# A lone tile's pass given ten load buffers and six split pairs, with the other tiles' first norm moved into routing

## The chip, the cores and the metric

One core of a Trainium2 chip runs the whole kernel. The metric is the device time of one execution in microseconds (us). Engines are called TensorE (PE in rows), VectorE (DVE), ScalarE (ACT), GpSimd (POOL) and the sync engine (SP), whose in-order queue issues nearly all weight loads. A name with a q behind it (SPq, ACTq) is an engine's queue of DMA issues and semaphore steps.

## The reference, cut to what matters

The input is 512 tokens of 2048 features in fp32, with 256 memory tokens. One layer is computed:

```python
h = rmsnorm(x, norm_mix_g); m = rmsnorm(mem, norm_mem_g)
z = h @ w_in                       # 2048 x 12288: u|v, conv B|C|h, queries, 3 x 2048 gates
y_A = u * (mask(W_s) @ LN(v) + b)  # u, v after gelu; per 128-token block
y_B = B * causal_conv3(C * h)
y_C = softmax(q k^T / 16) v        # 4 heads over the 256 memory tokens
x = x + (sum_n sigmoid(g_n) * (y_n @ w_branch[n])) @ w_out
h = rmsnorm(x, norm_ffn_g)
idx, g = product_key_top16(h @ w_q, keys)   # 8 heads x 16 of 16384 experts
x = x + sum_k g_k * gelu(w_down[idx_k] . h) * w_up[idx_k]
out = rmsnorm(x, norm_final_g)
```

## The kernel before, in words

Tokens are four tiles of 128. Every weight matrix streams from memory in units of 128 x 1024 fp32 (512 KB). `halves` (line 92) yields them. In the mixer each unit is split for an fp32-accurate product: ScalarE rounds `raw` to `whi` (line 111), VectorE subtracts to get `wlo` (line 112), and `mm3` (line 115) issues three matmuls, hi x hi, hi x lo and lo x hi, for each 128 rows of the unit. The tags `raw`, `whi` and `wlo` of the pool A have 4, 3 and 3 buffers. A load waits until the VectorE split has read the buffer that it reuses. In memory and routing the weights are not split (`raw=True`): there the fp32 unit goes to TensorE as it is, and its loads rotate through all three tags.

The order of the work is:

1. `memory` (line 227): keys and values of the 256 memory tokens, fp32 matmuls. In it `load_x(0)` (line 281) loads tile 0, squares it on ScalarE, multiplies by 1/rms and the gain on VectorE (line 298, gain broadcast to all partitions in `gb`), transposes it on TensorE (line 302) and splits it into `h0`.
2. `first_tile` (line 469): the lone tile's pass, called so because tile 0 goes through the mixer alone. Its tokens are the stationary operand and a weight row of 512 columns moves (`chainN`, line 175), six matmuls of 512 columns for each unit. The order is queries, attention, merge 2, gate input, u, merge 0, conv, merge 1, w_out: 272 units. In three places (`hooks`, lines 409, 413, 446) `load_x(1)`, `load_x(2)` and `load_x(3)` norm, transpose and split the other tiles into `hiT` and `loT`, 2 x 24 KB of each partition, in a pool `half` (H) that is open from the start. After w_out comes routing for tile 0 (line 509): four groups of eight w_q units, and after each group the scores and the top 16.
3. `other_tiles` (line 541): tiles 1 to 3 through the mixer together, from `hiT` and `loT`; then `retrieval` (routing and gates of the other tiles, down projections) and `experts` (line 806), whose up projections I call the up stage. There a pool `exp` gives two further buffers for each of `raw`, `whi` and `wlo`; before the change units 0 and 1 of each five took those. Beside stages 3 and later, single expert rows are gathered by GpSimd and multiplied on VectorE, paced by the units.

Every projection of the lone tile (line 317) ends with a ScalarE copy (line 327) of four 128-column chunks that TensorE then transposes (line 330). A scheduler fixes the order of the instructions on each engine and queue when the kernel is built, from the order in the program and modelled durations; on the chip each engine runs its list in order. Pools hand out a buffer when it is free in that plan.

Of the kernel before, what the change touches and what calls it, by code (L numbers as in the profile page):

```python
# [9 lines left out]
F32 = mybir.dt.float32  # L10
F32R = mybir.dt.float32r
# [4 lines left out]
AF = mybir.ActivationFunctionType  # L16
# [3 lines left out]
P = 128  # L20
# [42 lines left out]
class Builder:  # L63
    def __init__(self, ctx, tc, a):
        self.ctx, self.tc, self.nc, self.a = ctx, tc, tc.nc, a
        self.n_unit, self.n_down, self.extra = 0, 0, None
        self.gth, self.last_lo = None, None
# [24 lines left out]
    def halves(self, src, raw=False):  # L92


        nc, A = self.nc, self.A
        for u in range(src.shape[-1] // 1024):
            self.n_unit += 1
            if raw:
                tag, bufs = (("raw", 4), ("wlo", 3), ("raw", 4), ("wlo", 3), ("raw", 4), ("wlo", 3), ("raw", 4),
                             ("whi", 3))[self.n_unit % 8]  # L100
                w = A.tile([P, 1024], F32, tag=tag, name="unit", bufs=bufs)
                nc.sync.dma_start(w, src[:, bass.ts(u, 1024)])
                yield (w,)
# [5 lines left out]
            hi = pool.tile([P, 1024], F32R, tag="whi", name="whi", bufs=b or 3)  # L109
            lo = pool.tile([P, 1024], F32R, tag="wlo", name="wlo", bufs=b or 3)  # L110
# [83 lines left out]
    def consts(self):  # L194
        nc, A, a = self.nc, self.A, self.a
        self.ident = A.tile([P, P], F32, tag="ident", name="ident")
        make_identity(nc, self.ident)
        self.iota = A.tile([P, P], F32, tag="iota", name="iota")
        nc.gpsimd.iota(self.iota, pattern=[[1, P]], base=0, channel_multiplier=0,
                       allow_small_or_imprecise_dtypes=True)  # L200
        self.ss = A.tile([P, NT, 4], F32, tag="ss", name="ss")
        self.rg = A.tile([P, 1], F32, tag="rg", name="rg")
        self.fg = A.tile([P, KC], F32, tag="fg", name="fg")
        nc.scalar.dma_start(self.fg, a["ffn_g"])

    def small_operands(self):
# [20 lines left out]
    def memory(self):  # L227
# [24 lines left out]
        for c in range(WC):  # L252
# [20 lines left out]
            if c == 1:  # L273
                self.load_x(0)
        for c in range(2):
# [5 lines left out]
    def load_x(self, t):  # L281

        nc, A = self.nc, self.A
        x = self.rows("x", [P, D])
        nc.sync.dma_start(x, self.a["x"][bass.ts(t, P), :])
        if t == 0:
            self.gb = A.tile([P, D], F32, tag="hg", name="gb", bufs=1)
            nc.scalar.dma_start(self.gb, row_bcast(self.a["norm_mix_g"], D))
            self.h0 = [self.rows("h0", [P, KC, P], F32R) for _ in range(2)]
        elif t == 1:  # L290
            self.hiT = self.H.tile([P, KC, ND * P + P], F32R, tag="h", name="hiT", bufs=2)
            self.loT = self.H.tile([P, KC, ND * P + P], F32R, tag="h", name="loT", bufs=2)
        ss = self.small("sx", 4)
# [3 lines left out]
        r = self.rstd_of(ss[:, None, :])  # L297
        nc.vector.scalar_tensor_tensor(x, x, r, self.gb, op0=ALU.mult, op1=ALU.mult)
        for k4 in range(KC // 4):
            p = self.bank2("pt").rearrange("p (k t) -> p k t", k=4)  # L300
            for k in range(4):
                nc.tensor.transpose(p[:, k, :], x[:, bass.ts(k4 * 4 + k, P)], self.ident)
            hi, lo = self.h0 if t == 0 else (self.hiT, self.loT)
            s = (slice(None), slice(4 * k4, 4 * k4 + 4), bass.ts(max(t - 1, 0), P))
            self.split(hi[s], lo[s], p)


    def mixer(self, act, hooks):

# [60 lines left out]
        for h in range(HEADS):  # L370
# [32 lines left out]
            for c in range(2):  # L403
# [4 lines left out]
                put(2 * h + c, po)  # L408
        hooks[0]()
        merge(2, y, True)  # L410


        hooks[1]()
        vt = [M.tile([P, W], F32, tag="v", name="vt", bufs=4) for _ in range(nt)]
# [30 lines left out]

        hooks[2]()
        y, put = new_y()
# [21 lines left out]
    def first_tile(self):  # L469

        nc, A, a = self.nc, self.A, self.a
        act = Act(P, hi=lambda k: self.h0[0][:, k, :], lo=lambda k: self.h0[1][:, k, :])
        merged = self.mixer(act, [lambda: self.load_x(1), lambda: self.load_x(2), lambda: self.load_x(3)])
# [14 lines left out]
        for c in range(4):  # L488
# [52 lines left out]
    def other_tiles(self):  # L541
        nc, tc, A, a = self.nc, self.tc, self.A, self.a
        n = ND * P + P
        act = Act(n, hi=lambda k: self.hiT[:, k, :], lo=lambda k: self.loT[:, k, :])
        none = lambda: None
        merged = self.mixer(act, [none, none, none])
        self.gh = gh = self.H.tile([P, KC, n], F32R, tag="h", name="gh", bufs=2)
# [258 lines left out]
    def experts(self):  # L806
# [80 lines left out]
    def run(self):  # L887
        nc, tc = self.nc, self.tc
        self.h2h = None
        self.open()  # L890
        self.hpool, self.mpool = ExitStack(), ExitStack()
        self.H = self.hpool.enter_context(tc.tile_pool(name="half", bufs=1, side="right", reuse_waits="tile"))
        self.M = self.mpool.enter_context(tc.tile_pool(name="mix", bufs=1, side="left", reuse_waits="tile"))
# [26 lines left out]
def layout(inputs):  # L920
# [6 lines left out]
        "norm_mix_g": a["norm_mix_g"][0],  # L927
        "mem_g": cols(a["norm_mem_g"][0], KC),
        "ffn_g": cols(a["norm_ffn_g"][0], KC),
        "norm_ffn_g": a["norm_ffn_g"][0],  # L930
# [40 lines left out]
```

## Time and profile before

| | us |
|---|---|
| median of 3 runs | 4021.7 (4014.24 to 4022.86) |
| the profiled execution, its own time | 4022.7 |
| its span | 4020.8 |
| TensorE busy, whole span | 3603.0 (90%) |
| VectorE busy, whole span | 3157.9 (79%) |
| ScalarE busy, whole span | 1586.4 (39%) |
| lone tile's pass, first to last split matmul | 131.0 to 687.5 |
| routing of tile 0 | about 696 to 761 |

In rows of instructions the line comes first, then engine, operation, output<-inputs and shape; then busy us in total and mean ns of one; behind the bar the idle time of the engine just before them, with what ended it. TensorE's matmul rows are pipelined: the start of one and the next tell its pace, their lengths overlap.

### The profile page before, as it was taken

How to read it: one execution, taken by the hardware profiler on the slowest of the kernel's cores; microseconds unless marked ns; L12 is line 12 of the kernel's file. 1: busy time of each engine (PE TensorE's matmuls, PEld its weight loads, DVE VectorE, ACT ScalarE, POOL GpSimd, SP SyncE). 2: the span in 40 equal slices, each digit the busy share in tenths (PEclk: the TensorE clock that was granted, in tenths of full speed). 3: DMA queues.
4: the chain of work that ended last, by engine and by line, in shares of the span. 5: the costliest groups of instructions: out<-in, count | busy, mean ns of one | idle time of the engine just before them, and what ended most of it. 6: DMA issues, size and time to landing. Idle time of an engine off the chain costs nothing.

```text
span 4020.8 us, 52410 instructions
## 1 busy us (share of the span) xinstructions
PE 3603.0 (90%) x19846; PEld 3173.8 (79%) x19846; DVE 3157.9 (79%) x4050; ACT 1586.4 (39%) x2175; POOL 731.1 (18%) x544
## 2 busy tenths in 40 slices
PE   9888788989999999999689889999997788888888
PEld 6555555979999999998589888999997566666666
DVE  1566766588788888888897999888877787887887
ACT  1565655133233232323423355455433333333333
POOL 0000000022121132122200211222221222222231
PEclk9999999999999999999799999999998998999999
DMA  6587878589989999999754899999999989989996
GB/s 225 181 273 256 271 263 297 190 313 342 346 333 341 338 353 347 349 338 375 292 203 141 304 327 329 366 350 347 363 373 364 338 317 330 341 314 333 326 328 227
DMA packets 318653, 1240.83 MB, mean 309 GB/s; under 512 B 32704, under 2 KB 98240, under 8 KB 248768
## 3 DMA queue, kind: packets, MB, share of 16 engines
q1 hardware_dynamic: 242800, 692.16, 49.3%
q0 software_dynamic: 73728, 536.90, 35.2%
q10 hardware_dynamic: 1872, 8.43, 0.6%
q8 instruction: 155, 2.54, 0.2%
q14 instruction: 98, 0.80, 0.1%
HBM read 1198.56 MB, written 38.80 MB: 308 GB/s over the span
## 4 chain that ended last, share of the span: by engine, by line
PE 48%; DVE 21%; DMA 20%; issue 5%; ACT 5%; POOL 0%; ACTq 0%; SPq 0%; DVEq 0%; POOLq 0%
DVE wlo L112 9%; DMA raw<-in_w_upN 7%; DVE xg L777 4%; DMA raw<-in_w_restN 4%; ACT whi L111 4%; PE pg L117 3%; PE pg L118 3%; PE pg L119 3%; DMA raw<-in_w_downT 3%; PE pd L119 3%; PE po L118 3%; PE pd L117 3%; PE pd L118 2%; PE po L119 2%; PE po L117 2%
## 5 line engine op out<-in xcount | busy, mean ns | idle before, releaser
L111 ACT ACTIVATE whi<-raw 128x1024 fp32r<-128x1024 f32 x1096 | 1154.1, 1058 | 1873.6 <-DMA raw<-in_w_upN 347.7
L112 DVE TENSOR_TENSOR wlo<-raw,whi 128x1024 fp32r<-128x1024 f32 x1096 | 1335.0, 1222 | 461.2 <-ACT whi L111 457.4
L119 PE MATMUL pd<-h2h,wlo 128*128 128x256 f32 x2048 | 596.4, 291 | 46.3 <-DVE wlo L112 45.6
L774 POOL DMA_INDIRECT row<-in_w_down,eidx x256 | 333.3, 1302 | 1532.1 <-DVE row L779 976.1
L777 DVE SCALAR_TENSOR_TENSOR xg<-row,dots,xg 128x2048 f32<-128x2048 f32 x256 | 600.9, 2347 | 13.4 <-DMA row<-in_w_up,eidx 8.6
L779 DVE SCALAR_TENSOR_TENSOR row<-row,hg 128x2048 f32<-128x2048 f32 x256 | 585.0, 2286 | 25.3 <-DMA row<-in_w_down,eidx 25.1
L117 PE MATMUL pd<-h2h,whi 128*128 128x256 f32 x2048 | 591.6, 289 | 8.4 <-ACT ga L698 6.2
L774 POOL DMA_INDIRECT row<-in_w_up,eidx x256 | 385.0, 1504 | 1152.7 <-DVE xg L777 1042.5
L118 PE MATMUL pd<-h2l,whi 128*128 128x256 f32 x2048 | 585.7, 286 | 0.0
L118 PE MATMUL po<-wlo,aw 128*128 128x512 f32 x1024 | 430.5, 420 | 103.3 <-DVE wlo L112 102.9
L117 PE MATMUL po<-whi,aw 128*128 128x512 f32 x1024 | 395.8, 411 | 69.7 <-ACT whi L111 69.7
L119 PEld LDWEIGHTS pd<-h2h,wlo 128*128 128x128 f32 x2048 | 398.9, 195 | 65.0 <-DVE wlo L112 64.6
L119 PE MATMUL po<-whi,aw 128*128 128x512 f32 x1024 | 419.7, 410 | 0.0
L117 PEld LDWEIGHTS pd<-h2h,whi 128*128 128x128 f32 x2048 | 399.4, 195 | 10.8 <-ACT ga L698 7.4
L118 PEld LDWEIGHTS pd<-h2l,whi 128*128 128x128 f32 x2048 | 399.5, 195 | 0.0
L118 PEld LDWEIGHTS po<-wlo,aw 128*128 128x128 f32 x1024 | 205.1, 200 | 182.9 <-DVE wlo L112 140.3
L117 PEld LDWEIGHTS po<-whi,aw 128*128 128x128 f32 x1024 | 202.3, 199 | 122.8 <-ACT whi L111 79.0
L117 PE MATMUL pg<-hiT,whi 128*128 128x384 f32 x768 | 259.9, 338 | 2.0 <-ACT whi L111 2.0
L119 PE MATMUL pg<-hiT,wlo 128*128 128x384 f32 x768 | 259.8, 338 | 0.6 <-DVE wlo L112 0.6
L118 PE MATMUL pg<-loT,whi 128*128 128x384 f32 x768 | 259.3, 338 | 0.0
L119 PEld LDWEIGHTS po<-whi,aw 128*128 128x128 f32 x1024 | 204.9, 200 | 41.7
L124 DVE TENSOR_TENSOR aw<-ga,aw 128x256 fp32r<-128x256 f32 x128 | 53.9, 423 | 139.3 <-ACT aw L123 138.9
(352 smaller groups left out, 5912.6 us busy)
## 6 DMA issues: line engine op xcount, KB each, us to landing
raw<-in_w_downT SPq DMA_DIRECT2D x256, 512.0 KB, 6.6
raw<-in_w_upN SPq DMA_DIRECT2D x256, 512.0 KB, 7.1
raw<-in_w_restN SPq DMA_DIRECT2D x176, 512.0 KB, 5.0
raw<-in_w_rest SPq DMA_DIRECT2D x176, 512.0 KB, 6.9
raw<-in_w_out SPq DMA_DIRECT2D x72, 512.0 KB, 6.7
raw<-in_w_branchN SPq DMA_DIRECT2D x48, 512.0 KB, 5.4
raw<-in_w_branch SPq DMA_DIRECT2D x48, 512.0 KB, 7.5
raw<-in_w_gv SPq DMA_DIRECT2D x32, 512.0 KB, 5.9
```

Of the source, the lines that this page charges most:

```text
L111: nc.scalar.activation(hi, w, AF.Copy)
L112: self.last_lo = nc.vector.tensor_sub(lo, w, hi.bitcast(F32)).ins
L117: mm(out, lh, rh, start=start, stop=False)
L118: mm(out, lh, rl, start=False, stop=False)
L119: mm(out, ll, rh, start=False, stop=stop)
L124: (lo_engine or self.nc.vector).tensor_sub(lo, src, hi.bitcast(F32))
L774: nc.gpsimd.indirect_dma_start(out=row, out_offset=None, in_=self.a["w_up" if up else "w_down"], in_offset=bass.IndirectOffsetOnAxis(ap=g. ...
L777: nc.vector.scalar_tensor_tensor(g.x, row, g.dots[:, k:k + 1], g.x, op0=ALU.mult, op1=ALU.add)
L779: nc.vector.scalar_tensor_tensor(row, row, 1.0, g.hg, op0=ALU.mult, op1=ALU.mult, accum_out=g.dots[:, k:k + 1])
```

## The change

Before the first tile's pass a pool `first` is opened on the side and in the size (48 KB of each partition) of the two tiles `hiT` and `loT`; it holds six `raw` buffers and three pairs of `whi` and `wlo`. It is closed after the last w_out unit, and only then the pool for `hiT` and `loT` is opened. Units take the new pool's `raw` for 6 of each 10, and its split pairs for 3 of each 6. In the up stage the two numbers are 2 of each 6 for `raw` and 2 of each 5 for the splits.

`load_x` is cut in two. `load_x` itself loads and scales by 1/rms on ScalarE; `turn_x` transposes, multiplies by the gain on VectorE (gain now a value per partition, `mixg`), and splits. Tile 1 is loaded when w_out begins, into the second buffer of the tag y beside tile 0's x; tiles 2 and 3 are loaded in routing, into the same two buffers; tiles 1, 2 and 3 are turned after the first, second and third group of w_q units.

```diff
-            x = self.extra is not None and self.n_unit % 5 < 2
-            pool, b = (self.extra, 2) if x else (A, 0)
-            w = pool.tile([P, 1024], F32, tag="raw", name="raw", bufs=b or 4)
+            X, nr, ns = self.extra
+            pool, b = (X, nr) if self.n_unit % (nr + 4) < nr else (A, 4)
+            w = pool.tile([P, 1024], F32, tag="raw", name="raw", bufs=b)
             nc.sync.dma_start(w, src[:, bass.ts(u, 1024)])
+            pool, b = (X, ns) if self.n_unit % (ns + 3) < ns else (A, 3)
...
             if c == 1:
-                self.load_x(0)
+                x = self.load_x(0)
+            if c == 3:
+                self.turn_x(0, x)
...
     def load_x(self, t):
-        x = self.rows("x", [P, D])
+        x = self.rows("x", [P, D]) if t == 0 else A.tile([P, D], F32, tag="y", name="x", bufs=2)
...
-        nc.vector.scalar_tensor_tensor(x, x, r, self.gb, op0=ALU.mult, op1=ALU.mult)
+        for c in range(4):
+            xs = x[:, bass.ts(c, 512)]
+            nc.scalar.activation(xs, xs, AF.Copy, scale=r)
+        return x
+
+    def turn_x(self, t, x):
...
         for k4 in range(KC // 4):
             p = self.bank2("pt").rearrange("p (k t) -> p k t", k=4)
             for k in range(4):
-                nc.tensor.transpose(p[:, k, :], x[:, bass.ts(k4 * 4 + k, P)], self.ident)
-            self.split(hi[s], lo[s], p)
+                self.nc.tensor.transpose(p[:, k, :], x[:, bass.ts(k4 * 4 + k, P)], self.ident)
+            ks = slice(4 * k4, 4 * k4 + 4)
+            h = self.tmp("h3").rearrange("p (k t) -> p k t", k=4)
+            self.nc.vector.tensor_tensor(h, p, self.mixg[:, ks, None].to_broadcast([P, 4, P]), op=ALU.mult)
+            s = (slice(None), ks, bass.ts(max(t - 1, 0), P))
+            self.split(hi[s], lo[s], h)
...
         mh, ml = (self.rows("m0", [P, KC, P], F32R) for _ in range(2))
+        xs1 = self.load_x(1)
...
         nc.sync.dma_start(self.xdram, x)
+        self.xpool.close()
+        self.extra = None, 0, 0
+        self.H = self.hpool.enter_context(self.tc.tile_pool(name="half", bufs=1, side="right", reuse_waits="tile"))
...
+        xs = [None, xs1, self.load_x(2), None]
         for h4 in range(4):
             pq = self.bank("pq")
             for s in range(4):
                 self.whole(pq[:, bass.ts(s, P)], a["w_q"][4 * h4 + s], act)
+            if h4 < 3:
+                self.turn_x(h4 + 1, xs[h4 + 1])
+            if h4 == 0:
+                xs[3] = self.load_x(3)
...
-            self.extra = L
+            self.extra = L, 2, 2
...
+        X = self.xpool.enter_context(tc.tile_pool(name="first", bufs=1, side="right", reuse_waits="tile"))
+        self.extra = X, 6, 3
```

The three hooks of the mixer are taken out.

## Rows read from the trace of the kernel before

**Rows 1.** Busy time by stretch: engines' busy us (count), clock, DMA share, GB/s.

```profile
10.00:20.00 10.00, 8.10 (x36) 6.25 (x35) 6.68 (x19) 4.83 (x8) 0.00 (x0) 0.83 1.03 412
...
131.00:688.00 557.00, 457.73 (x1810) 326.47 (x1808) 386.13 (x447) 337.61 (x418) 4.39 (x16) 0.97 0.80 264
...
696.00:761.00 65.00, 62.09 (x542) 61.33 (x542) 16.36 (x98) 7.31 (x12) 0.00 (x0) 0.99 0.70 234
3080.00:3960.00 880.00, 731.68 (x2877) 566.32 (x2878) 719.00 (x733) 295.25 (x368) 230.61 (x126) 0.93 0.91 329
```

**Rows 2.** Chain that ended last, 632 to 660: start us, length, what.

```profile
634.61 5.01 DMA raw<-in_w_out
...
639.73 1.07 ACT whi L111
640.82 1.24 DVE wlo L112
642.07 4.77 DMA raw<-in_w_out
```

**Rows 3.** Waits of the sync queue, 131 to 688: total us, times, longest.

```profile
SPq L108 <- DVE wlo L112: 376.7, 236, 9.3
```

**Rows 4.** Timeline of TensorE, 669 to 671.6: start us, length, instruction.

```profile
669.06 0.39 PE L118 MATMUL po<-wlo,m 128*128 128x512 f32 x1
...
671.55 0.39 PE L117 MATMUL po<-whi,m 128*128 128x512 f32 x1
```

**Rows 5.** Instruction groups by form, 131 to 688, TensorE (columns: section above).

```profile
L118 PE MATMUL pg<-wlo,h 128*128 128x512 f32 x192 | 82.0, 427 | 20.9 <-DVE wlo L112 20.0
...
L383 PE MATMUL sc<-kT,qT 128*128 128x256 f32 x16 | 5.1, 449 | 0.0
L406 PE MATMUL po<-pT,vm 128*128 128x128 f32 x32 | 4.5, 283 | 0.7 <-ACT pT L402 0.7
L436 PE MATMUL sv<-wT,vt 128*128 128x128 f32 x16 | 3.3, 373 | 0.0
...
L330 PE MATMUL put<-ident,pur 128*128 128x128 f32 x8 | 1.8, 361 | 6.8 <-ACT pur L327 6.8
```

**Rows 6.** Timelines of TensorE, memory (29 to 33) and routing (728 to 744).

```profile
28.64 2.75 PE L167 MATMUL pk<-mT,unit 128*128 128x256 f32 x12
31.44 1.09 PE L302 MATMUL pt<-ident,x 128*128 128x128 f32 x8
...
728.04 1.16 PE L517 MATMUL sc<-keys,qT 128*128 128x128 f32 x8 [0.69 <-ACT qT L514]
729.04 14.46 PE L167 MATMUL pq<-hgT,unit 128*128 128x128 f32 x128
```

**Rows 7.** DMA queues, 131 to 688: packets, MB, share of 16 engines.

```profile
q1 hardware_dynamic: 39329, 144.79, 78.3%
```

**Rows 8.** Instruction groups by form, 131 to 688, VectorE and ScalarE.

```profile
L112 DVE TENSOR_TENSOR wlo<-raw,whi 128x1024 fp32r<-128x1024 f32 x269 | 327.3, 1224 | 148.0 <-ACT whi L111 145.1 <-PE pb L119 0.2
L111 ACT ACTIVATE whi<-raw 128x1024 fp32r<-128x1024 f32 x269 | 283.4, 1058 | 205.6 <-DMA raw<-in_w_restN 79.9 <-DMA raw<-in_w_branchN 28.0 <-DMA raw<-in_w_out 21.1
...
L295 ACT ACTIVATE junk<-x 128x512 bf16<-128x512 f32 x12 | 7.4, 616 | 0.0
L298 DVE SCALAR_TENSOR_TENSOR x<-x,r,gb 128x2048 f32<-128x2048 f32 x3 | 7.0, 2349 | 0.1
```

**Rows 9.** Lines 596, 590: duration ns min/median/max, first and last start us.

```profile
L596 DVE TENSOR_TENSOR h<-pt,fg x12: 684/691/692, 1963.0 to 2001.9; 128x512 f32<-128x512 f32 x12
...
L590 ACT ACTIVATE h<-x,r x12: 705/706/722, 1961.1 to 1998.4; 128x512 f32<-128x512 f32 x12
```

**Rows 10.** Waits of the sync queue, 3080 to 3960.

```profile
SPq L108 <- DVE wlo L112: 238.6, 127, 7.1
```

**Rows 11.** DMA issues, 3080 to 3960: count, KB each, median us to landing.

```profile
raw<-in_w_upN SPq DMA_DIRECT2D x238, 512.0 KB, 7.1
```

More of the change, by code (lines that the diff above doesn't have):

```diff
@@ L65, in __init__ @@
         self.ctx, self.tc, self.nc, self.a = ctx, tc, tc.nc, a
-        self.n_unit, self.n_down, self.extra = 0, 0, None
+        self.n_unit, self.n_down, self.extra = 0, 0, (None, 0, 0)
         self.gth, self.last_lo = None, None
@@ L104, in halves @@
                 continue
-            x = self.extra is not None and self.n_unit % 5 < 2
-            pool, b = (self.extra, 2) if x else (A, 0)
-            w = pool.tile([P, 1024], F32, tag="raw", name="raw", bufs=b or 4)
+            X, nr, ns = self.extra
+            pool, b = (X, nr) if self.n_unit % (nr + 4) < nr else (A, 4)
+            w = pool.tile([P, 1024], F32, tag="raw", name="raw", bufs=b)
             nc.sync.dma_start(w, src[:, bass.ts(u, 1024)])
-            hi = pool.tile([P, 1024], F32R, tag="whi", name="whi", bufs=b or 3)
-            lo = pool.tile([P, 1024], F32R, tag="wlo", name="wlo", bufs=b or 3)
+            pool, b = (X, ns) if self.n_unit % (ns + 3) < ns else (A, 3)
+            hi = pool.tile([P, 1024], F32R, tag="whi", name="whi", bufs=b)
+            lo = pool.tile([P, 1024], F32R, tag="wlo", name="wlo", bufs=b)
             nc.scalar.activation(hi, w, AF.Copy)
@@ L204, in consts @@
         nc.scalar.dma_start(self.fg, a["ffn_g"])
+        self.mixg = A.tile([P, KC], F32, tag="mixg", name="mixg")
+        nc.scalar.dma_start(self.mixg, a["mix_g"])
     def small_operands(self):
@@ L283, in load_x @@
         nc, A = self.nc, self.A
-        x = self.rows("x", [P, D])
+        x = self.rows("x", [P, D]) if t == 0 else A.tile([P, D], F32, tag="y", name="x", bufs=2)
         nc.sync.dma_start(x, self.a["x"][bass.ts(t, P), :])
[L286 to L292, printed above, removed]
         ss = self.small("sx", 4)
@@ L297, in load_x @@
         r = self.rstd_of(ss[:, None, :])
-        nc.vector.scalar_tensor_tensor(x, x, r, self.gb, op0=ALU.mult, op1=ALU.mult)
+        for c in range(4):
[3 more added lines that the diff above has]
+    def turn_x(self, t, x):
+        if t == 0:
+            hi, lo = self.h0 = [self.rows("h0", [P, KC, P], F32R) for _ in range(2)]
+        elif t == 1:
+            self.hiT = self.H.tile([P, KC, ND * P + P], F32R, tag="h", name="hiT", bufs=2)
+            self.loT = self.H.tile([P, KC, ND * P + P], F32R, tag="h", name="loT", bufs=2)
+        if t > 0:
+            hi, lo = self.hiT, self.loT
         for k4 in range(KC // 4):
@@ L301, in load_x, with mixer @@
             for k in range(4):
-                nc.tensor.transpose(p[:, k, :], x[:, bass.ts(k4 * 4 + k, P)], self.ident)
-            hi, lo = self.h0 if t == 0 else (self.hiT, self.loT)
-            s = (slice(None), slice(4 * k4, 4 * k4 + 4), bass.ts(max(t - 1, 0), P))
-            self.split(hi[s], lo[s], p)
-    def mixer(self, act, hooks):
+                self.nc.tensor.transpose(p[:, k, :], x[:, bass.ts(k4 * 4 + k, P)], self.ident)
[4 more added lines that the diff above has]
+            self.split(hi[s], lo[s], h)
+    def mixer(self, act):
         nc, A, M, a = self.nc, self.A, self.M, self.a
@@ L408, in mixer @@
                 put(2 * h + c, po)
-        hooks[0]()
         merge(2, y, True)
-        hooks[1]()
         vt = [M.tile([P, W], F32, tag="v", name="vt", bufs=4) for _ in range(nt)]
@@ L443, in mixer @@
         merge(0, y, False)
-        hooks[2]()
         y, put = new_y()
@@ L472, in first_tile @@
         act = Act(P, hi=lambda k: self.h0[0][:, k, :], lo=lambda k: self.h0[1][:, k, :])
-        merged = self.mixer(act, [lambda: self.load_x(1), lambda: self.load_x(2), lambda: self.load_x(3)])
+        merged = self.mixer(act)
         x = A.tile([P, D], F32, tag="y", name="x0", bufs=2)
@@ L544, in other_tiles @@
         act = Act(n, hi=lambda k: self.hiT[:, k, :], lo=lambda k: self.loT[:, k, :])
-        none = lambda: None
-        merged = self.mixer(act, [none, none, none])
+        merged = self.mixer(act)
         self.gh = gh = self.H.tile([P, KC, n], F32R, tag="h", name="gh", bufs=2)
@@ L890, in run @@
         self.open()
-        self.hpool, self.mpool = ExitStack(), ExitStack()
-        self.H = self.hpool.enter_context(tc.tile_pool(name="half", bufs=1, side="right", reuse_waits="tile"))
+        self.hpool, self.mpool, self.xpool = ExitStack(), ExitStack(), ExitStack()
+        X = self.xpool.enter_context(tc.tile_pool(name="first", bufs=1, side="right", reuse_waits="tile"))
+        self.extra = X, 6, 3
         self.M = self.mpool.enter_context(tc.tile_pool(name="mix", bufs=1, side="left", reuse_waits="tile"))
@@ L928, in layout @@
         "mem_g": cols(a["norm_mem_g"][0], KC),
+        "mix_g": cols(a["norm_mix_g"][0], KC),
         "ffn_g": cols(a["norm_ffn_g"][0], KC),
```

## The prediction, made before the changed kernel was run

> **What bounds the kernel now.** I read the busy time by stretch first, then the waits of the sync queue, the chain of waits, the groups of instructions by form, and short timelines.
>
> The lone tile's pass runs from the first w_restN matmul at 131.0 us to the last w_out matmul at 687.5 us: 556.5 us. In that stretch no engine and no queue is full: TensorE is shown busy 82%, VectorE 69%, ScalarE 61%, DMA share 0.80 at 264 GB/s [rows 1]. What repeats is a loop through four load buffers. The chain shows it unit by unit: a load of 5.01 us, its ScalarE split of 1.07, its VectorE split of 1.24, and at once the next load into the buffer just released, 7.46 us after the one before [rows 2]. Four buffers in 7.46 us are 1.87 us a unit, 281 GB/s. The sync queue confirms it: its weight loads wait 376.7 us in 236 waits for the VectorE split that empties their buffer [rows 3]. The pass has 272 units of 512 KB (from the code: 80 for projections and gate input, 144 in the three merges, of which 48 branch units, 16 more for queries and 32 of w_out), so it runs at 2.05 us a unit; 0.18 of that is other waits.
>
> How far it can fall is set by the next limits. TensorE: a unit is six matmuls of 512 columns, and twelve of them issue 2.49 us apart from first to last, eleven intervals of 0.2264 us [rows 4]; 272 x 6 x 0.2264 = 369.5 us. Its other work is scores, attention output and spatial gating, at most 5.1 + 4.5 + 3.3 us by their busy rows [rows 5], and 64 transposes at 1.09/8 = 0.136 us [rows 6], 8.7 us: 391 us with those. The 48 transposes of the other tiles are another 6.5. So TensorE is really idle 556.5 - 391 - 6.5 = 159 us, not the 99 us that its busy row leaves.
>
> The Trainium skill (Perfetto Trace Analysis, Identifying the Most-Contended Engine) says that matmul busy time is a poor measure of headroom because matmuls are pipelined, and sends the reader to weight-load time. The trace agrees: rows of 390 ns start every 0.226 us, and weight loads fill 59% of the stretch. By the busy row alone the pass could lose at most 99 us.
>
> Loads: the queue moves 144.79 MB in the pass [rows 7], two of them for x tiles 2 and 3, and at 412 GB/s, which the first units of the kernel reach with the same 4 KB rows and more buffers [rows 1], this takes 351 us. VectorE has 386 us busy [rows 1], less 19 for what leaves it (three multiplies of 2.35, twelve half-size splits of some 0.7 and small operations): 367 us. So behind the buffer limit stand TensorE at 391, VectorE at 367 and the loads at 351.
>
> **The change part by part.**
>
> Buffers in the pass. Load buffers go from 4 to 10, split pairs from 3 to 6, in even rotation (6 of 10 and 3 of 6 in the new pool). The loop of 7.46 us then allows 0.75 us a unit, so the wait for a load buffer is gone as a limit and loads lengthen until another limit holds. The split pairs would have been next: a pair is held for 1.06 + 1.22 [rows 8] + 6 x 0.226 = 3.64 us and some hand-overs, over three 1.2 to 1.3 us, over six 0.6. What is late next is TensorE. It also starts with more units ready, since ten loads and six splits can wait for it during the memory stage, where it is fully busy.
>
> New length of the pass: 391 us of TensorE work, plus ten places where a projection is copied by ScalarE before it is transposed. Each costs at least what the same copy costs in routing, 0.69 us [rows 6], and about half a split queued ahead: 12 us together. That is 403 us, the low end. High end: half of the remaining idle time stays (159 - 12 = 147, half 74): 477 us. I take 430 us, 1.58 us a unit: 143 MB in that time is 332 GB/s, next to the 329 GB/s which this kernel holds over 880 us of its up stage, where three resources are as evenly loaded as they will be here [rows 1]. Gain 126 us, between 79 and 153.
>
> The Trainium skill (HBM Reference, Specifications (TRN2)) gives a core some 358 GB/s as its share of a memory that two cores use, and more when it streams alone. By the share the loads alone would need 400 us, just above TensorE, and I would put the pass at about 440, 10 us less gain. The trace speaks against the share here: 412 GB/s over 10 us.
>
> Norms of tiles 1 to 3 taken out of the pass. Per tile that is one VectorE multiply of 2.35 us, four ScalarE squares of 0.62 [rows 8], splits, 16 transposes and a 1 MB load. VectorE and ScalarE hide it once they aren't the limit, so it is already in the figures above; TensorE's 6.5 us were left out of the 391. One tile (1) comes back at the pass's end, its load beside that of tile 0: both wait for the last branch's y, and behind them on the sync queue wait w_out loads. 1 MB is 2.5 us at 412 GB/s; loads already issued into ten buffers cover it. On ScalarE four squares and four scaled copies of 0.71 [rows 9] fall among 32 splits: 32 x 1.06 + 5.3 and the rest is near TensorE's 43.5 us. I leave it within the 27 us allowed above 403.
>
> Turning tiles 1 to 3 during routing. Routing is TensorE-bound: groups of 128 fp32 matmuls in 14.46 us, nothing between them but a 0.69 us wait for the copy before the scores [rows 6]. Each tile adds 16 transposes, 2.2 us, in two PSUM buffers. The third four wait for the VectorE multiply by the gain, 0.69 us [rows 9], and that and the split (0.69 more, as the multiply) make about 1.3 us per four: 2.5 to 4 us a tile. The 0.69 us wait is then filled. Three tiles: +8 us. VectorE's own 12 multiplies and 12 splits, 17 us, lie in time in which it is a quarter busy [rows 1]. Low end 0, if the transposes fall into gaps. High end +35: the load of tile 3 waits until tile 1 is transposed, and if w_q loads stand behind it on the in-order sync queue, TensorE finds its buffers empty for a load's length, 5 to 8 us at each of three places.
>
> The first tile in the memory stage: its gain is now applied after the transposes, on VectorE, beside TensorE-bound matmuls; a 1 MB broadcast load goes and an 8 KB one comes. I take 0, +-2 us, since the eight transposes stand between matmuls with no gap [rows 6]. Opening the other tiles' space later: its first writer comes in routing, its first reader after, 0; without that cover it would be one release wait, under 1 us.
>
> Up stage. The same lines now rotate loads there through 6 of 6, where before two in five units had a distance of 5 and the others of 6 to 8. The queue is in order, so the effective depth goes from about 5.6 to 6. Its loads wait 238.6 us for a split to empty a buffer [rows 10] and take 7.1 us [rows 11]; DMA is at 0.91, VectorE at 82% [rows 1]. 7% more depth on those 238.6 us is 17 us at most unless the stage reorders; against DMA's remaining 9%, I take -12. Ends: -35 (DMA share from 0.91 to 0.95 over 880 us) and +15 (the gathers and the small loads are squeezed by earlier weight loads).
>
> Sum: -126 + 8 - 12 = -130 us. The profiled execution took 4022.7 us (span 4020.8): 4022.7 - 130 = 3892.7; the median of the three runs is 1.0 lower, so 3892 us.
>
> **The rivals.**
> A. The buffers deepen but the orders written at build time, or loads and TensorE limits that nearly coincide, keep half or more of the idle time. For it: at 1.36 us a unit the loads would have to run at 385 GB/s, 94% of the best row, and VectorE would be 85% full (367 of 430) with splits that depend on ScalarE. Against: six pairs are 8 us of lead. Pass 477 to 500, routing +15, up -5: 3935 to 3965, say 3948.
> B. All limits are met: pass 403 to 410, up stage -30, routing +5: about 3848.
> C. Slower. Engines run in a fixed order. With six pairs free, splits of later units may be queued on ScalarE ahead of the copies, sigmoids and exponentials that TensorE waits for. Up to six splits are 6.4 us; there are 38 such places (10 copies, 12 sigmoids, some 16 of attention and gating). From 3.4 us each the gain of 130 is gone; at 5 us it is 190 us, so 4080. For it: a copy's wait is already 6.8 us in two places [rows 5]. Against: those waits arise now because the splits ahead wait for loads, which end.
> D. The change doesn't do what it says: loads lengthen in proportion to their number, the rate stays at 264 GB/s and the pass at some 550, routing +8, up stage -5: about 4020. For it: the DMA share is 0.80 already. Against: even 264/0.80 = 330 GB/s gives a pass of 433, as forecast, and the 412 GB/s row more.
>
> **How the numbers follow.** Forecast 0.62, A 0.22, B 0.09, C 0.05, D 0.02. A measurement of this kernel tells about 0.2%, 8 us, from no change. Faster: forecast, A and B, 0.93; same: D, 0.02; slower: C, 0.05. The forecast's own range is 3860 to 3930; to hold 8 in 10 it reaches through B's 3848 and most of A: 3848 to 3962.
>
> **What would show it.** Right: sync queue's waits for the VectorE split in the pass fall below 150 us; loads there take 8 us or more instead of 5; the pass is 410 to 455 us at 315 to 350 GB/s; TensorE's waits for the VectorE split, 20.9 us on the gate matmuls alone [rows 5], fall to a third. Routing grows from 65 to 70 to 78 us with no gap of 5 us before w_q matmuls. The up stage is 0 to 30 us shorter. Wrong: the pass above 480 us, or the sum of waits on ScalarE's copies above 50 us (C), or TensorE idle in routing behind w_q loads, or the time between 131 and 761 us giving less than 70 us.

## The result, and the profile after

The changed kernel takes 3862.5 us (median of 4 runs, 3860.7 to 3865.3), the kernel before beside it 4018.0 us. The ratio is 0.9615, with an interval of 0.9597 to 0.9634. The forecast was 3892 us: the sign and the range held, and the gain is 155.5 us where 130 was forecast.

The two profiled executions, whose spans differ by 160.8 us, cut at the same instructions (the first matmul of each stage), show where the time went:

| stage, us | before | after | difference | forecast |
|---|---|---|---|---|
| memory | 131.0 | 128.0 | -3.0 | 0, +-2 |
| lone tile's pass | 556.5 | 422.6 | -133.9 | -126 |
| end of the pass to routing | 8.5 | 7.6 | -0.9 | 0 |
| routing | 65.3 | 79.4 | +14.1 | +8 |
| other tiles' mixer | 1235.2 | 1246.7 | +11.5 | 0 |
| retrieval and down stage | 1062.5 | 1057.1 | -5.4 | 0 |
| last down matmul to first up matmul | 21.6 | 9.7 | -11.9 | 0 |
| up stage | 940.2 | 908.9 | -31.3 | -12 |
| span | 4020.8 | 3860.0 | -160.8 | -130 |

The busy time by stretch of the changed kernel (columns as in [rows 1]): the pass, its end, routing, and the other tiles' mixer.

```profile
128.00:551.00 423.00, 406.45 (x1762) 319.64 (x1760) 353.84 (x415) 307.07 (x385) 6.26 (x16) 0.99 0.92 332
551.00:558.00 7.00, 3.38 (x15) 3.04 (x16) 4.20 (x12) 2.46 (x6) 0.00 (x0) 0.66 0.91 303
558.00:638.00 80.00, 71.08 (x596) 69.14 (x596) 34.40 (x137) 25.33 (x51) 0.00 (x0) 0.94 0.66 224
638.00:1884.00 1246.00, 1198.06 (x6432) 1141.13 (x6430) 1046.78 (x1088) 395.69 (x496) 290.01 (x255) 0.98 0.89 332
```

The first row answers to the pass in [rows 1]. The loads ran at 264 GB/s and now run at 332, TensorE is shown busy 96% instead of 82%, and the DMA share went from 0.80 to 0.92.

What ends last in the pass is told by the chain of waits, its shares by line. First the kernel before, 131 to 688 us:

```profile
by line: DMA raw<-in_w_restN 27.6%; DVE wlo L112 15.9%; ACT whi L111 14.5%; DMA raw<-in_w_branchN 11.0%; DMA raw<-in_w_out 7.9%; issue 5.2%; DMA raw<-in_w_gv 3.1%; ACT junk L295 1.0%; PE pg L117 1.0%; PE pg L118 1.0%; PE pg L119 0.8%; PE pb
```

and the changed kernel, 128 to 551 us:

```profile
by line: PE pg L119 8.5%; PE pg L120 8.1%; PE pg L118 7.8%; PE pb L119 5.4%; PE pb L120 5.3%; PE pb L118 5.2%; issue 4.8%; DVE wlo L113 4.8%; ACT whi L112 4.3%; DMA raw<-in_w_out 2.7%; PE po L119 2.6%; PE po L120 2.5%; PE po L118 2.5%; PE p
```

Before, the loop of load, ScalarE split and VectorE split made up 80% of the chain (loads 49.6, splits 30.4). After, TensorE leads it: its pieces make up 77% of the whole chain (the line shows the largest groups), and those of all loads 4%. TensorE is the bound, as forecast. One part differs. At about 500 us w_out's units follow two tiles of x in the sync queue, and there the chain passes through a load of 11.25 us, issued at 499.33 us: from 505 to 515 us TensorE is busy 5.58 of 10 us, while the DMA share is 1.00. In the 20 us behind that the loads still run at 410 to 413 GB/s, but TensorE is busy all the time:

```profile
505.00:515.00 10.00, 5.58 (x14) 3.63 (x14) 4.77 (x11) 9.85 (x17) 0.00 (x0) 0.83 1.00 376
515.00:525.00 10.00, 10.00 (x44) 7.92 (x44) 10.00 (x11) 9.85 (x12) 0.00 (x0) 1.00 1.02 413
525.00:535.00 10.00, 10.00 (x45) 8.18 (x44) 8.91 (x9) 6.90 (x10) 0.00 (x0) 1.00 1.03 410
```

Waits of the sync queue in the pass of the changed kernel (answers to [rows 3]):

```profile
SPq L108 <- DVE wlo L113: 235.3, 222, 5.0
```

and the loads issued there (count, KB each, median us from issue to landing):

```profile
raw<-in_w_restN SPq DMA_DIRECT2D x160, 512.0 KB, 6.4
raw<-in_w_branchN SPq DMA_DIRECT2D x48, 512.0 KB, 6.2
raw<-in_w_out SPq DMA_DIRECT2D x32, 512.0 KB, 8.4
```

TensorE's groups by form in the pass (answers to [rows 5]): the wait of the gate matmuls for the VectorE split, 20.9 us before, is 2.0.

```profile
L119 PE MATMUL pg<-wlo,h 128*128 128x512 f32 x192 | 77.3, 402 | 2.0 <-DVE wlo L113 1.7
```

### The profile page after: what moved, and what is told of

Its sections match the earlier page's. It is cut to its first block, busy times and chain, and to the rows that moved or that the text cites. A ratio compares the mean times of both kernels' runs of the same rounds, so it can differ in the third digit from the quotient of the medians.

```text
span 3860.0 us, 52453 instructions
## 1 busy us (share of the span) xinstructions
PE 3547.0 (92%) x19846; PEld 3168.8 (82%) x19846; DVE 3145.8 (81%) x4062; ACT 1582.2 (41%) x2186; POOL 745.4 (19%) x544
## 4 chain that ended last, share of the span: by engine, by line
PE 59%; DVE 19%; DMA 14%; issue 5%; ACT 3%; POOL 0%; SPq 0%; DVEq 0%; ACTq 0%; POOLq 0%
DMA raw<-in_w_upN 7%; DVE wlo L113 7%; PE pg L119 4%; PE pg L120 4%; PE pg L118 4%; PE po L119 3%; DVE xg L795 3%; PE po L120 3%; PE pd L120 3%; PE po L118 3%; DMA raw<-in_w_downT 3%; PE pb L119 3%; PE pd L118 3%; PE pb L120 3%; PE pb L118 3%
## 5 line engine op out<-in xcount | busy, mean ns | idle before, releaser
L792 POOL DMA_INDIRECT row<-in_w_down,eidx x256 | 342.4, 1338 | 1511.5 <-DVE row L797 972.9
L118 PE MATMUL po<-whi,aw 128*128 128x512 f32 x1024 | 391.8, 406 | 68.5 <-ACT whi L112 58.9
L120 PE MATMUL po<-whi,aw 128*128 128x512 f32 x1024 | 414.5, 405 | 0.0
L702 ACT ACTIVATE Aw<-Aw,ratio 128x128 fp32r<-128x128 f32 x256 | 86.6, 392 | 174.6 <-DVE Aw L700 174.5
```

Of the source, the lines that this page charges most:

```text
L118: mm(out, lh, rh, start=start, stop=False)
L120: mm(out, ll, rh, start=False, stop=stop)
L702: nc.scalar.activation(A[:, z, 1, :], A[:, z, 0, :].bitcast(F32), AF.Copy, scale=ratio[:, t0 + z:t0 + z + 1])
L792: nc.gpsimd.indirect_dma_start(out=row, out_offset=None, in_=self.a["w_up" if up else "w_down"], in_offset=bass.IndirectOffsetOnAxis(ap=g. ...
```

## The experiments

Each kernel is the changed one with one edit, unless said otherwise. "Stage" times come from its profiled execution, cut as in the table; ratios are to the kernel before on the same chip.

### Which half of the change made the pass shorter

**No buffers.** `self.extra = X, 6, 3` becomes `None, 0, 0` in `run`: four load buffers and three split pairs in the pass, all else as changed.

> The changed kernel without the ten and six: the norms stay moved into routing, but the pass has the 4 load buffers and 3 split pairs of before. Buffer theory: the pass (first to last split matmul) stays at 540 to 556 us, its loads land in 5 us, the sync queue waits over 300 us for splits; routing keeps its 14 us more and the up stage its gain: 3975 to 3998 us. Rival, a good part of the 134 us came from taking three norms out of the pass: pass below 520, kernel 3960 or less.

**Load buffers alone.** `self.extra = X, 6, 0`.

> The changed kernel with the six more load buffers, but the 3 split pairs of before. Load-buffer theory: most of the gain is there, pass 440 to 475 us against 423, kernel 3878 to 3915, since three pairs held for 3.64 us and hand-overs allow about 1.3 us a unit without slack. Rival, the split pairs are the second half of the limit: pass 480 to 520 us, kernel 3920 to 3960.

**Split pairs alone.** `self.extra = X, 0, 3`.

> The pass keeps the four load buffers of before and gets six pairs of split buffers; all else as in the changed kernel. Theory (the number of loads in flight sets the pace, a split buffer is worth nothing by itself): the pass takes 535 to 556 us, as with no buffers (548.3), and the time is 3975 to 3995 us. Rival (the split buffers carry part of the gain by themselves, and the loads' run showed little without them only because either one suffices): the pass takes under 490 us and the time is under 3935 us.

**Six load buffers instead of ten.** `self.extra = X, 2, 3`.

> Six load buffers in the pass instead of ten, six pairs of split buffers. Theory (a cycle of four buffers takes some 7.5 us, so six would already be over what the DMA engines moved at ten; from there the DMA engines are the limit): the pass takes 425 to 455 us, the time is 3865 to 3900 us. Rival (each buffer is worth the same, 548 - 423 over six buffers, 21 us each): the pass takes 495 to 515 us, the time is 3935 to 3955 us. Two load buffers in the up stage's rotation are not part of this run: only the pass changes.

The pass, one row from each kernel (columns as in [rows 1]): no buffers, split pairs alone, six load buffers, load buffers alone.

```profile
129.80:678.10 548.30, 453.04 (x1762) 322.61 (x1760) 370.68 (x418) 324.48 (x388) 6.34 (x16) 0.96 0.80 264
```
```profile
129.70:666.30 536.60, 451.27 (x1762) 324.01 (x1760) 367.38 (x416) 322.55 (x387) 6.26 (x16) 0.96 0.81 270
```
```profile
132.70:566.10 433.40, 410.00 (x1762) 316.98 (x1760) 357.75 (x414) 317.38 (x385) 6.29 (x16) 0.99 0.93 329
```
```profile
131.30:559.60 428.30, 407.37 (x1762) 316.99 (x1760) 365.93 (x417) 324.51 (x388) 6.15 (x16) 0.99 0.92 331
```

| load buffers / split pairs | pass, us | time, us (ratio, interval) |
|---|---|---|
| 4 / 3 | 548.3 | 3989.2 (0.9940, 0.9917 to 0.9963) |
| 4 / 6 | 536.6 | 3983.6 (0.9925, 0.9896 to 0.9954) |
| 6 / 6 | 433.4 | 3882.9 (0.9656, 0.9627 to 0.9685) |
| 10 / 3 | 428.3 | 3873.2 (0.9650, 0.9620 to 0.9680) |
| 10 / 6 | 422.6 | 3862.5 (0.9615, 0.9597 to 0.9634) |

The load buffers are the cause. With four of them the pass stays at 537 us or more whatever the split pairs are; three more pairs are worth 6 to 12 us in both lines. Two load buffers more already give 103 of the 114 us between four and ten. Moving the norms out of the pass may be worth some 8 us by itself (556.5 to 548.3; in two further kernels with the pass of before it takes 557 and 561 us). The rival that each buffer is worth the same is refuted: six reached 433 us where it asked for 495 to 515. Load buffers alone came out better than the theory's own range, 428 us against 440 to 475.

That the DMA engines are the limit from six buffers on, as the last expectation has it, is not shown: their share is 0.93 with six and 0.92 with ten, and TensorE leads the chain with ten. Counted from the issue and the landing of each load, more than six loads are under way for only 16 of the 422.6 us with ten buffers.

### The up stage's rotation

**The old rotation there, all else as changed:** `n_unit % (nr + 4)` becomes `n_unit % (nr + (3 if nr == 2 else 4))`.

> The changed kernel with one thing undone: in the up stage load buffers rotate as before (units 0 and 1 of each five in the extra pool). If the rotation of load buffers made the up stage 43 us shorter (from the last down matmul to the end: 962 us before, 919 after), that stretch goes back to 950 to 970 us and the kernel takes 3890 to 3915 us. Rival, the up stage gained because the shorter pass shifted gathers and orders: the stretch stays at 910 to 930 and the kernel within 12 us of 3862.

**The kernel before with the new rotation of loads alone:** its load buffers go to the second pool where `n_unit % 6 < 2`, its split pairs where `n_unit % 5 < 2`, as they did.

> The kernel before with the new rotation of load buffers in the up stage (units 0 and 1 of each six; splits as before) and nothing else. Rotation theory: last down matmul to end falls from 962 to 915 to 930 us, the kernel to 3965 to 3990. Rival (shifted orders): no change, 4010 to 4024.

With the old rotation the changed kernel takes 3893.6 us (0.9721, 0.9705 to 0.9737); the kernel before with the new one takes 3984.2 us (0.9944, 0.9927 to 0.9960). So the edit is worth 1.06% by the difference of the first ratio to that of the changed kernel, 42 us, and 0.56%, 22 us, when it is made alone. The profiles agree on the place: between the last down matmul and the first up matmul pass 21.6 and 21.3 us with the old rotation and 10.1 and 9.7 with the new one, and the up stage falls from 940.2 and 929.9 to 915.7 and 908.9.

The gap and the up stage, first the kernel before:

```profile
3059.00:3080.60 21.60, 0.30 (x3) 0.10 (x1) 9.93 (x15) 4.92 (x8) 2.62 (x2) 0.59 0.92 314
3080.60:4020.80 940.20, 778.90 (x3072) 604.26 (x3072) 757.97 (x787) 317.33 (x407) 230.61 (x126) 0.93 0.89 318
```

then the changed one:

```profile
2941.40:2951.10 9.70, 0.23 (x2) 0.03 (x1) 4.21 (x6) 1.79 (x4) 0.94 (x1) 0.74 1.06 350
2951.10:3860.00 908.90, 762.82 (x3072) 595.92 (x3072) 764.61 (x797) 325.57 (x413) 235.33 (x127) 0.94 0.92 333
```

In the gap, VectorE ran 15 instructions before and 6 after. The chain of the kernel before passes there through a load of gathered activations, issued at 3066 us:

```profile
3066.33 10.40 DMA ga<-adram
```

In the changed kernel that load is not on the chain ahead of the first up matmul; the chain goes from the sync queue's issues straight into a weight load of 7.52 us. The two kernels of this section agree: with the old rotation the chain passes through such a load, of 11.92 us, and with the new one alone it does not. Gap and up stage together are 33 and 36 us shorter by these profiles, beside the 42 and 22 us of the times. Why the rotation alters this order was not tried by itself. In the stage behind it, the sync queue's wait for the VectorE split is 221.7 us where the old rotation in the changed kernel has 246.4.

### Routing, and the other tiles' pace

The changed kernel's routing, TensorE in the first of four turns (answers to the second half of [rows 6]):

```profile
573.40 1.04 PE L313 MATMUL pt<-ident,x 128*128 128x128 f32 x8
574.79 1.25 PE L313 MATMUL pt<-ident,x 128*128 128x128 f32 x8 [0.35 <-DVE h L316]
576.27 0.63 PE L313 MATMUL pt<-ident,x 128*128 128x128 f32 x4 [0.23 <-ACT hiT L124]
578.72 0.63 PE L313 MATMUL pt<-ident,x 128*128 128x128 f32 x4 [1.82 <-DVE h L316]
583.85 2.08 PE L536 MATMUL sc<-keys,qT 128*128 128x128 f32 x8 [4.50 <-ACT qT L533]
```

and ScalarE in the same turn:

```profile
580.75 0.63 ACT L293 ACTIVATE junk<-x 128x512 bf16<-128x512 f32 x1 [1.52 <-DMA x<-in_x]
...
582.61 0.61 ACT L293 ACTIVATE junk<-x 128x512 bf16<-128x512 f32 x1
583.13 0.19 ACT L293 ACTIVATION_READ_ACCUMULATOR junk<-x 128x1 f32 x1
583.22 0.57 ACT L533 ACTIVATE qT<-pq 128x512 f32<-128x512 f32 x1
```

ScalarE's queue holds the four squares of tile 3 ahead of the copy that the scores need. The squares wait for tile 3's load, and TensorE waits 4.50 us for the copy. From its first w_q matmul to that of the next, the four turns take 27.5, 17.9, 17.8 and 16.2 us; in the kernel before they take 16.9, 16.1, 16.1 and 16.2. So 10.5 of the 14.1 us lie in the first turn, and the second and third tile cost 1.7 us each.

A part of the first turn is the granted clock. From 580.6 to 587.4 us it is 0.50, the lower of its two levels (1.2 GHz), after TensorE was busy 3.55 of the 7.20 us before. The eight score matmuls above take 2.08 us there, and 1.16 in the kernel before [rows 6]. In the run with two edits below, the clock is 1.00 at this place.

In the other tiles' mixer TensorE is idle for 47 to 48 us in both kernels, and its matmuls are the same (6432 and 6435 recorded), but eight intervals of 128x384 matmuls take 1.39 us before and 1.41 us after. Over all intervals of the stage that are shorter than 0.25 us, some 5290 in each kernel, the mean is 0.1736 us before and 0.1754 after; every kernel with the changed kernel's buffers has the slower pace, and the kernel before with the new rotation has the faster. What these two families differ in is the place of the buffers in memory: the gain tile `mixg`, 64 bytes per partition, stands ahead of the weights' buffers and moves them, `wlo` from byte 43040 to 43104. (The expectations below give the pace as 0.1733 and as 0.1748 to 0.1760 us; those are means of shorter stretches.)

**The gain tile from the other pool:** `self.mixg = A.tile(` becomes `self.mixg = self.M.tile(`.

> The changed kernel with the 64 bytes per partition of the norm's gain taken from another pool, so that the weights' load and split buffers begin where they began before (wlo at 43040, not 43104), only whi still lies elsewhere than before. Theory (the start of the weights' buffers sets the matmuls' pace): the 128x384 matmuls of the other tiles come every 0.1733 us again instead of 0.1748 to 0.1760, that stage takes 1232 to 1237 us instead of 1247, the time is 3848 to 3855 us. Rival (whi's place, or something that the buffers' start has no part in): pace, stage and time as in the changed kernel, 3858 to 3866 us.

**The kernel before with 64 bytes more:** behind `fg`, `pad = A.tile([P, KC], F32, ...)` and one load into it, which nothing reads.

> The kernel before with one more tile of 64 bytes per partition (and one small load into it), which nothing reads: every buffer behind it moves by 64 bytes, and nothing else changes. Theory (the start of the weights' buffers sets the pace): the 128x384 matmuls come every 0.1748 to 0.1760 us instead of 0.1733, the other tiles take 1244 to 1247 us instead of 1235, the time is 10 to 12 us above the kernel before. Rival (something else of the change slows them): pace and time as before, within 3 us.

Eight intervals of the same matmuls, first and ninth start; the kernel before:

```profile
1479.70 0.34 PE L118 MATMUL ph<-loT,whi 128*128 128x384 f32 x1
...
1481.09 0.34 PE L117 MATMUL ph<-hiT,whi 128*128 128x384 f32 x1
```

the kernel before with the pad, at the same time of its span:

```profile
1479.67 0.34 PE L118 MATMUL ph<-loT,whi 128*128 128x384 f32 x1
...
1481.09 0.34 PE L117 MATMUL ph<-hiT,whi 128*128 128x384 f32 x1
```

The mixer of the padded kernel, to be held against the changed kernel's 1198.06 us of TensorE and DMA share 0.89 at 332 GB/s above:

```profile
760.40:2005.60 1245.20, 1198.40 (x6436) 1140.59 (x6434) 1047.19 (x1089) 396.52 (x497) 286.75 (x255) 0.98 0.89 332
```

The pad alone, with no other edit, takes the mean pace to 0.1754 us and the stage from 1235.2 to 1245.2 us; the time is 4024.1 us, a ratio of 1.0021 (1.0002 to 1.0040). Moving the gain tile brings the pace back to 0.1736 and the stage to 1238.5 us. Its time, 3863.7 us (0.9610, 0.9582 to 0.9638), lies in the rival's range and cannot be told from the changed kernel's: 8 us are about what the measurement resolves, and other stages came out longer in its profile. So the place of what stands behind the tile sets the pace, shown in both directions by the pace and the stage.

**32 and 96 bytes:** the gain tile in the other pool and a tile of 32, or of 96, bytes per partition in its old place.

> The changed kernel with the gain tile in the other pool and one tile of 32 bytes per partition in the place where it was: the weights' buffers begin 32 bytes later than in the kernel before (wlo at 43072). Theory (it is the place modulo some power of two over 64 bytes that sets the pace, and 64 bytes off is the worst of the places): a pace between 0.1733 and 0.1755 us for 128x384 matmuls, the other tiles 1236 to 1247 us, the time 3855 to 3863. Rival (the place that the kernel before has is itself a slow one): the pace falls under 0.170 us, the other tiles take under 1215 us and the time is under 3835 us. No third theory says which.

> As the run with 32 bytes, but 96: the weights' buffers begin at a multiple of 128 bytes (wlo at 43136 = 337 x 128). Theory (a multiple of 128 is a place as good as the one of the kernel before): 0.1733 us for 128x384 matmuls, the other tiles 1235 to 1239 us, the time 3850 to 3858. Rival (only a start away from that of the moving operands' tiles helps, or a multiple is better than all): under 0.170 us and under 3835 us. If the pace is 0.1748 or more, it is the distance from the place of before that counts and not the multiple.

Both theories and both rivals fell. The time is 3873.7 us (0.9643, 0.9617 to 0.9669) at 32 bytes and 3870.3 us (0.9634, 0.9609 to 0.9659) at 96. The mean interval in ns, of all 128x384 matmuls and of two products apart:

| bytes later | gates (`pg`, moving `hiT`, `loT`) | branches (`pb`, moving `yh`, `yl`) | all | stage, us |
|---|---|---|---|---|
| 0, kernel before | 173.4 | 173.9 | 173.6 | 1235.2 |
| 0, gain tile moved | 173.4 | 174.0 | 173.6 | 1238.5 |
| 32 | 176.6 | 173.8 | 175.5 | 1248.3 |
| 64, kernel before with pad | 176.1 | 173.7 | 175.4 | 1245.2 |
| 64, changed kernel | 176.1 | 173.7 | 175.4 | 1246.7 |
| 96 | 176.7 | 174.7 | 176.1 | 1246.5 |

Of the four places tried, the one that the kernel before had is the best, and a multiple of 128 bytes is no better than the others; the length of the stage does not tell 32, 64 and 96 apart. At 32 and 64 bytes the gates are slower and the branches are not, although both take their stationary weights from the same `whi` and `wlo`. So the place of the weights' buffers alone does not set the pace; it differs with the tile that moves. Which of the moved tiles counts was not tried apart, and why is open.

**Three edits together:** the gain tile moved; in each turn of routing, the lines below behind the copy of the scores; and in the last column products of the pass, the load of x of tile 0 behind the first column's weight loads, of tile 1 behind the second's.

```
-            if h4 < 3:
-                self.turn_x(h4 + 1, xs[h4 + 1])
-            if h4 == 0:
-                xs[3] = self.load_x(3)
             qT = self.tmp("qT")
...
             nc.scalar.activation(sv, sc, AF.Copy)
+            if h4 < 3:
+                self.turn_x(h4 + 1, xs[h4 + 1])
+            if h4 == 0:
+                xs[3] = self.load_x(3)
```

> Three edits of the changed kernel at once, each read in its own stage. (1) The gain tile from the other pool (weights' buffers where they began before). (2) In routing, tile 3's load and squares and the transposes of the next tile stand behind the scores of the turn, not ahead of them. (3) x of tile 0 is asked for after the first column of w_out's loads, x of tile 1 after the second, and the first column's sum waits for it, so that the sync queue does not stop ahead of w_out's loads. Theory: (1) other tiles 1235 to 1239 us instead of 1247; (2) ScalarE's four squares stood ahead of the copy that the first scores need, 4.5 us of a wait, and now stand behind it: routing 72 to 76 us instead of 79; (3) the pause of the matmuls at the start of w_out goes: pass 416 to 420 us instead of 423. Together 3840 to 3852 us. Rival: routing's 14 us are the moved instructions' own time on TensorE and the copies between the transposes, wherever they stand: routing 78 to 81 us; and the pass is set by the loads' rate, so that a pause of the matmuls at w_out is made good behind it: pass 421 to 425 us. Together 3855 to 3860 us.

**The first two of them:**

> The first two edits of the run with three (the gain tile from the other pool; tile 3's load and squares and the next tile's transposes behind the scores of the turn), without the third: x of tiles 0 and 1 is asked for where the changed kernel asks for it. Theory (the order in the turn alone gave routing's 11 us back, and moving the loads of x gave nothing): routing 67 to 70 us, the pass 421 to 426 us, the time as with all three, 3842 to 3853 us. Rival (the later loads of x had a part in it, since tile 1's x then came into the end of the pass and not ahead of it): routing 71 to 80 us, the time 3852 to 3865 us.

With three edits: 3849.1 us (0.9578, 0.9553 to 0.9603), routing 68.0, mixer 1235.0, pass 424.8 us. With two: 3849.7 us (0.9580, 0.9556 to 0.9604), routing 68.5, mixer 1234.2, pass 421.4 us. TensorE in the first turn with two edits:

```profile
574.81 0.82 PE L313 MATMUL pt<-ident,x 128*128 128x128 f32 x6
575.66 1.16 PE L532 MATMUL sc<-keys,qT 128*128 128x128 f32 x8
576.66 0.38 PE L313 MATMUL pt<-ident,x 128*128 128x128 f32 x2
576.88 0.83 PE L168 MATMUL pq<-hgT,unit 128*128 128x128 f32 x6
```

The scores start 0.85 us after the first of these transposes instead of 10.45, and transposes run among the next turn's matmuls. Routing gives back 10.9 of its 14.1 us; the rival that the moved work costs that time wherever it stands is refuted.

The third edit gave nothing, as its rival said, but it did not do what it was meant to. In the changed kernel the sync queue stops for 9.7 us ahead of most of w_out's loads, and TensorE idles 2.80 us at 507.7. With the edit two more of these loads go out, and then the queue stops as long at another place, for the landing of the load of `keys`:

```profile
SPq L108 <- DMA keys<-in_keysT: 9.9, 1, 9.9
```

The stop ends at 499.91 us, 0.06 us after `keys` has landed. The load that waits signals its landing on the same semaphore as the load of `keys`: the traces show eight such semaphores for the DMAs that SyncE and ScalarE issue, with 187 or 188 of them on each. In the changed kernel `keys` lands at 497.46 us, so that this wait is hidden behind the one for x. With the edit TensorE idles 3.70 us at 526.3, while ScalarE's squares (520.0 to 525.2 us) stand ahead of its next split. So whether the pass gains when w_out's loads start without a stop is not shown.

The version with two edits is the best simple one. On one chip, the kernel with three edits took 3842.3 to 3851.0 us and those with the gain tile moved to the 32- and 96-byte places 3865.1 to 3877.5, without overlap. The difference of the medians to the 32-byte one is 24.6 us, and the two stages give 11.4 + 13.3. Against the changed kernel, 0.9580 to 0.9615 is about 14 us, with intervals that overlap a little.

## Why the prediction was right, and where it was not

**The pass** (-126 forecast, -133.9 measured). The reading of the loop was right: four buffers in 7.46 us were the limit, behind it stood TensorE, and the pass came to 332 GB/s, the very rate that was taken. That it came so near is in part luck, since two terms were off in opposite directions. TensorE's own work was put too low: the 0.2264 us came from twelve matmuls at one place, and over all intervals of the pass shorter than 0.26 us the mean is 0.2308 (0.2303 in the kernel before). That makes 377 us of 369.5 and 398 of 391, and leaves some 25 us of idle time where 39 were allowed. The ten copies were put too high: TensorE waits 6.4 us for them, not 12. That loads already issued would cover the load of x at the start of w_out was wrong as well: five were out, the queue stopped for 9.7 us, and TensorE waited 4.5 us. The busy row of before, 457.73 of 557 us [rows 1], would have allowed a gain of 99 us at most; the measured 134 shows that matmul starts, not busy time, give the headroom. The Trainium skill (Perfetto Trace Analysis, Identifying the Most-Contended Engine) says that matmul busy time is a poor measure of headroom; the trace agrees.

**Two of the signs that should show it were wrong.** (Two more were missed narrowly: routing's 79.4 us lie above 70 to 78, and the up stage's 31.3 above 0 to 30.) The sync queue's waits were to fall below 150 us and the loads to take 8 us or more; they fell from 376.7 to 235.3 us, and projection and branch loads took 6.2 to 6.4 us. Both rested on one error: that the loads would lengthen until the buffers' cycle was full of them. At 1.55 us a unit (422.6 over 272 units) ten buffers go round in 15.5 us. Of these 6.4 are the load and 2.3 the two splits, so that by this estimate a loaded buffer only waits for its turn for some 6.8 us: the limit is behind it, on TensorE. The queue issues in order and so still waits 235 us for buffers with ten of them. Its wait tells that the consumer is slower, not that buffers are short; the length of the load beside the cycle does.

**The split pairs.** The forecast said that they "would have been next" with three. With ten load buffers three pairs cost 5.7 us more pass than six: the hold time of 3.64 us over three pairs, 1.2 us, stays under the 1.55 that the pass needs. Right in kind, small in size.

**Routing** (+8 forecast, +14.1 measured). The step that failed is "the 0.69 us wait is then filled": in the first turn it became 4.50 us. The 16 transposes were costed with their waits, but ScalarE's squares of tile 3 were not placed: they stand ahead of the copy that releases the scores, and wait for a load. This is the mechanism of rival C, instructions ahead of a copy in a queue of fixed order, at one place instead of 38 and with squares instead of splits. The tiles that did not meet it cost 1.7 us each, less than the 2.5 to 4 us forecast. Rows of w_q loads, named as the upper end, did not matter.

**The other tiles** (0 forecast, +11.5 measured). No term of the sum held it. The new gain tile was counted as one load of 8 KB and not as 64 bytes ahead of the weights' buffers.

**The up stage** (-12 forecast, -43.2 with the gap ahead of it). This is the mis-sized term. It was worked out as depth, 5.6 to 6 buffers in effect. The DMA share did go only from 0.89 to 0.92, but the rate went from 318 to 333 GB/s and the stage became 31 us shorter, close to the -35 that was kept for it as an end; the 11.9 us of the gap lay outside it, since the start of the stage was not looked at.

The errors partly cancel. Against the forecast the spans differ by +6 in routing and +11.5 in the mixer, -9 in the three rows forecast as 0 ahead of routing and in retrieval and down stage, -31 in the gap and the up stage and -8 in the pass: -31 together. Memory's -3.0 us lie outside the +-2, but kernels with the same memory stage reach its end between 127.9 and 132.7 us, so that no term can be named for it. Rivals A, C and D are refuted by the pass of 422.6 us (A's own parts add up to 3952 to 3975 us, not to 3935 to 3965); B named 3848 us, which the version with two edits reaches by another road.

The Trainium skill's share of a core (HBM Reference, Specifications (TRN2)), some 358 GB/s, would by the forecast's estimate have put the pass at 440 us. It took 422.6 at 332 GB/s on average, and stretches of 10 us ran at 410 to 413: no run here shows a ceiling at the share. What the Trainium skill says in the same section of a core that streams alone, that it gets more than the share, fits these stretches.

## What to carry to other kernels

When a stage is a loop through load buffers, divide the loop's length by the number of buffers and compare it with what the next engine needs by its start-to-start times; buffers beyond that crossing (here six: 6.0 us of load and 2.3 of splits over six are 1.38 us, against the 1.46 that TensorE's 398 us make over 272 units) bring little, 11 us for the last four against 103 for the first two. When work is moved into another stage, look in each engine's queue for what it now stands ahead of: the move cost 14 us, and 11 of them went when the same instructions were put behind the copy that TensorE needed. When an edit should take a wait away, look whether another wait ends at the same time: here the stop of the sync queue stayed. Start and end of a stage need a look of their own when a rotation is altered.

## What the runs showed of the hardware that was not expected

A tile of 64 bytes per partition that nothing reads slowed the 128x384 matmuls of a stage from 173.6 to 175.4 ns on average by moving the buffers behind it, at a granted clock of 0.98 for the stage in both; 32 and 96 bytes gave 175.5 and 176.1. It is not all matmuls: at 64 bytes those that move `hiT` and `loT` in the gates went from 173.4 to 176.1, and those that move `yh` and `yl` stayed at 173.7 to 173.9, with the same weights' buffers. In a stage of 1235 us this is 10 to 13 us. The matmuls of 512 columns in the pass hardly differed (0.2308 us in the changed kernel, 0.2303 before).

The wait for a completion semaphore can hold an in-order queue as a missing buffer does: a load of w_out stood 9.9 us behind the landing of a 1 MB load from another queue that signals on the same one.
